# Convolution taps on the vector engine: their place in the issue order behind operations of their own step

## The chip, the cores and the metric

The kernel runs on one core of a Trainium2 chip. Its time is the device time of one execution in microseconds (us). Three runs of the kernel before gave 1438.69, 1437.74 and 1432.52 us; the median is 1437.74 us. TensorE (PE in the profile) multiplies matrices into PSUM, VectorE (DVE) and ScalarE (ACT) empty PSUM and do elementwise work, GpSimd (POOL) does elementwise work in SBUF, SyncE (SP) issues most DMAs. Each engine runs its own instructions in the order in which they were put into its program.

## The reference, cut to what matters

The kernel computes a two-layer block on 512 tokens (and 256 context tokens in its first layer), followed by a second block with two attentions and a mixture of 32 experts. Only the two layers of the first block are touched. In each of them a wide input projection of the normalised tokens feeds an attention branch and two convolution branches, which an output projection joins again:

```python
parts = split_in(h @ w_in[l])
q = mla_q(parts[0], ...)
k, v = mla_kv(parts[1], parts[2], ...)
attn = attend(q, concat([kc, k]), concat([vc, v]))          # 8 heads
y_a = attn * silu(g_a)
y_b = sc_b * dwconv(sc_c * sc_in, sc_conv_w) * silu(g_b)    # 3 taps
z = dwconv(a * sigmoid(g), cf_conv_w) + cf_conv_b           # 31 taps, 256 channels
z = silu(layer_norm(z, cf_ln_w, cf_ln_b))
y_c = (z @ cf_pw_w + cf_pw_b) * silu(g_c)
x_new = x + gate * (concat([y_a, y_b, y_c]) @ w_out[l])
```

Layer 0 does this for 768 rows (512 tokens and 256 context rows), layer 1 for 512 rows and uses the context for keys and values only. All of it is float32; a large product is three matmuls of a high and a low part of each factor (`mm3`, lines 219 to 221), so most operands are split first: ACT makes the high part, DVE the low one (`split`, lines 182 and 183).

## The kernel before, in words

The 256 channels of the 31-tap convolution are two tiles `zp` of 128 channels each. A tap is one DVE instruction over a whole row (783 columns in layer 0, 512 in layer 1): line 566 for the first tap, line 569 for the other thirty, which multiply a shifted row by a weight column and add the sum so far, `za`. So a layer has 62 taps, and the taps of one tile form a chain. They go into a list `taps` when the projection `cf_g` of their tile is done, and `tick(n)` takes n of them from the list and writes them into the program.

A layer has two loops around them. The **token loop** runs over six tiles of 128 rows. For each it projects keys, values and queries, takes their norms (`rsq`, ten small DVE operations in a chain, lines 231 to 240), scales the keys `kt` (line 850) and the queries `qt` (line 855) and stores both to DRAM. In between, `early.run` hands out matmuls of eight projections: `cf_a` and `cf_g` of both tiles and the four attention gates `g_a`. A gate's PSUM bank is emptied by a tanh on ACT (line 528) and a multiply on DVE (line 529). These projections use two PSUM banks in turn. After each tile stands `tick(TA)`, and one more after the loop. The list is empty in the first tile; it gets its first taps in the second.

The **attention loop** runs over (head, group of 256 queries): 24 steps in layer 0, 16 in layer 1. A step takes scores (`pS`), their maximum on DVE (line 917), the exponential on ACT, the reciprocal on DVE, a multiply on POOL (line 921), transposes on TensorE and a split of each into two parts (lines 182 and 183), and the product with the values in `pO`. It ends with the DVE operation `ot` (line 965), which adds the two halves of `pO`, and with a POOL multiply into `oa` (line 966). `late.run` hands out matmuls of ten further projections (the 3-tap branch, the gates `g_b` and `g_c`, one PSUM bank) and of the modulation weights. Then stands `tick(TB)`. From three quarters of the steps on (step 18 and step 12, counted from 0) `tick(99)` writes all taps that are left, and the layer norm of the convolution begins (`norm_conv`, its first matmul `pmean` on line 637).

In this part of the kernel the order on each engine isn't the order of the text. A scheduler goes through the whole block with modelled durations and gives each engine, when it is free, the earliest instruction of the text that is ready by its model. So a tap that is ready can be put ahead of much that stands before it in the text, whenever DVE would have to wait for that. The order is fixed at build time; on the chip each engine just follows it. In the second block PE's order is written by hand (`manual_schedule`), in places ACT's and DVE's too.

Of the kernel before, what the change touches and what calls it, by code (L numbers as in the profile page):

```python
# [15 lines left out]
OP = mybir.AluOpType  # L16
# [64 lines left out]
        self.debt = min(self.debt, 2.0)  # L81


TA, TB, PB, LNS = 3, 2, 4, 0.75
FP = (0.9, 0.9)
FF = (0.3, 0.2, 0.3)
PTB = 3
# [23 lines left out]
class K:  # L111
# [356 lines left out]
    def layer(self, l, hT, wl):  # L468

        nc, I, sp, tc = self.nc, self.I, self.sp, self.tc  # L470
# [24 lines left out]
        for nm in ("q_head_norm_w", "k_head_norm_w"):  # L495
            w = self.brow(tr, I[nm][l][64:96], 32, "w32" + nm[0])
            t = tr.tile([128, 4, 2, 32], F32, name="tab" + nm[0])
# [40 lines left out]
        za, zs, taps = [None] * 2, [None] * 2, []  # L538
# [32 lines left out]
            taps.extend((tap, k) for k in range(31))  # L571

        def tick(n):
            for _ in range(min(n, len(taps))):
                f, k = taps.pop(0)
                f(k)

        def g_a(i):
            yield from cm(416 + i * 128, gate2(oa[:, i, :NTOK]), self.p1)
# [104 lines left out]
        for t in range(6):  # L684
            if t < 5:
                parts[t + 1] = self.qkv_cT(t + 1, *lat[t + 1][:2], tr, qnw, kvnw, last)
            self.qkv_tile(l, t, lat[t][0], lat[t][2], parts[t], tr, qtm, ktm, vtm, tabs, last)
            early.run(8 * sum(n for _, n in segs) / 800 * 4 / 3)
            tick(TA)
        early.run(1e9)  # L690
        tick(TA)
        tr.release()

# [9 lines left out]
        n = len(mods) // 4  # L703
# [29 lines left out]
        for s, (h, g) in enumerate(steps):  # L733
            if g == 0 and h + 1 < H:
                prep[h + 1] = self.mla_prep(h + 1, ap, qtm, ktm, vtm, qk, last)
            out = self.mla_out(h, g, prep[h][0], Ps, ap, oa)
            if s + 1 < len(steps):
                h1, g1 = steps[s + 1]
                if g1 == 0:
                    for _ in prep[h1][1]:  # L740
                        pass
                Ps = self.mla_scores(prep[h1][0], g1, ap)
            next(out)
            sh = each * (0.5 if g == 2 else 1.0)
            late.run(sh * FF[0])
            for _ in out:
                late.run(sh * FF[1])
            if h + 1 < H:
                for _ in range(2):
                    next(prep[h + 1][1], None)  # L750
            late.run(sh * FF[2])
            if last and s % 2:
                self.table_rows(s // 2)
            tick(TB)
            late.level()
            if g == ngr - 1 and h % 2:
                halves.append(h // 2)
            over = not (late.gens or late.ready)
            if s >= len(steps) * LNS and (over or stage < 4):
                tick(99)  # L760
                next(ln, None)
                stage += 1
            if over:
                next(tail, None)
                for i in halves:
                    self.split(hT[0][:, i, :NTOK], hT[1][:, i, :NTOK], oa[:, i, :NTOK])
                halves = []
# [42 lines left out]
    def qkv_tile(self, l, t, L, kss, cT, tr, qtm, ktm, vtm, tabs, last):  # L810
        nc, sp = self.nc, self.sp
        isx = t < 4
        doq = isx or not last
        ch, cl = cT
        st = sp.tile([128, 16], F32, name="hst", bufs=2)
        kt = tr.tile([128, 8, 96], F32, name="kt", tag="kt", bufs=2)
        vs = tr.tile([128, 8, 64], F32, name="vs", tag="vs", bufs=1)
        pk = self.pa("pkv")
        for s in range(2):
            self.mm3(pk[:, s * 512:(s + 1) * 512], (ch[:, 2], cl[:, 2]),  # L820
                     [w[:, s * 512:(s + 1) * 512] for w in self.wukv], True, True)
        pkv = pk.rearrange("p (h n) -> p h n", h=8)
        nc.scalar.activation(kt[:, :, 0:64], pkv[:, :, 0:64], AF.Copy)
        nc.scalar.activation(vs, pkv[:, :, 64:128], AF.Copy)
        nc.sync.dma_start(vtm[t].rearrange("p (h n) -> p h n", h=8), vs)
        if doq:
            qt = tr.tile([128, 8, 96], F32, name="qt", tag="qt", bufs=2)
            pq = self.pa("pq")
            for c0, c1 in ((0, 512), (512, 768)):
                for k in range(2):  # L830
                    self.mm3(pq[:, c0:c1], (ch[:, k], cl[:, k]), [w[:, c0:c1] for w in self.wuq[k]], k == 0, k == 1)
            nc.scalar.activation(qt, pq[:, :768].rearrange("p (h n) -> p h n", h=8), AF.Copy)
        sk = tr.tile([128, 768], F32, name="sq", tag="sq", bufs=2)[:, :512].rearrange("p (h n) -> p h n", h=8)
        nc.scalar.activation(sk, kt[:, :, 0:64], AF.Square)
        nc.vector.tensor_reduce(st[:, 8:16], sk, axis=AX.X, op=OP.add)
        nc.vector.tensor_scalar(st[:, 8:16], st[:, 8:16], kss, None, op0=OP.add)
        r = sp.tile([128, 16], F32, name="hr", bufs=2)
        if doq:
            sqq = tr.tile([128, 768], F32, name="sq", tag="sq", bufs=2).rearrange("p (h n) -> p h n", h=8)
            nc.scalar.activation(sqq, qt, AF.Square)  # L840
            nc.vector.tensor_reduce(st[:, 0:8], sqq, axis=AX.X, op=OP.add)
            self.rsq(r, st, 1.0 / 96, EPS)
        else:
            self.rsq(r[:, 8:16], st[:, 8:16], 1.0 / 96, EPS)
        kr = L[:, 384:416]
        if isx:
            kk = sp.tile([128, 2, 32], F32, name="krot", bufs=2)
            self.rope_op(kk, kr[:, None, :], tabs[1][:, t], 1, tr)
            kr = kk[:, 0, :]
        nc.vector.tensor_tensor(kt[:, :, 0:64], kt[:, :, 0:64], r[:, 8:16, None].to_broadcast([128, 8, 64]), op=OP.mult)  # L850
        nc.gpsimd.tensor_tensor(kt[:, :, 64:96], kr[:, None, :].to_broadcast([128, 8, 32]),
                                r[:, 8:16, None].to_broadcast([128, 8, 32]), op=OP.mult)
        nc.sync.dma_start(ktm[t].rearrange("p (h n) -> p h n", h=8), kt)
        if doq:
            nc.vector.tensor_tensor(qt, qt, r[:, 0:8, None].to_broadcast([128, 8, 96]), op=OP.mult)
            if isx:
                self.rope_op(None, qt[:, :, 64:96], tabs[0][:, t], 8, tr)
            nc.sync.dma_start(qtm[t].rearrange("p (h n) -> p h n", h=8), qt)
# [66 lines left out]
    def mla_out(self, h, g, qkv, Ps, ap, oa):  # L925

        nc = self.nc
        v = qkv["v"]
        nj = 2 if g == 2 else 6
        def tr(j):  # L930
            p = self.pt("pPT").rearrange("p (j n) -> p j n", j=2)
            for jj in range(2):
                for i in range(2):
                    nc.tensor.transpose(p[:, jj, i * 128:(i + 1) * 128], Ps[i][:, (j + jj) * 128:(j + jj + 1) * 128],  # L934
                                        self.ident)
            x = [ap.tile([128, 2, 256], F32R, name="PT" + k, tag="PT" + k, bufs=PTB) for k in "hl"]
            self.split(*x, p)
            return x

        def pv(j, x):  # L940

            for k in range(2):
                for jj in range(2):
                    nc.tensor.matmul(pO, v[:, (4 if g == 2 else 0) + j + jj, :], x[k][:, jj, :],
                                     start=(j + k + jj == 0), stop=(j + 2 == nj and k + jj == 2))

        pO = self.po("pO")[:, :256]
        t0 = tr(0)
        if g == 2:
            yield  # L950
            pv(0, t0)
        else:
            t1 = tr(2)
            yield
            pv(0, t0)
            t2 = tr(4)
            yield
            pv(2, t1)
            yield
            pv(4, t2)  # L960
        b = (h % 2) * 64
        o = oa[b:b + 64, h // 2, g * 256:(g + 1) * 256]
        t = ap.tile([128, 256], F32, name="ot", tag="ot", bufs=2)[b:b + 64]
        nc.scalar.activation(t, pO[64:128], AF.Copy)
        nc.vector.tensor_tensor(t, pO[0:64], t, op=OP.add)  # L965
        nc.gpsimd.tensor_tensor(o, o, t, op=OP.mult)  # L966


# [1197 lines left out]
```

## Time and profile before

| | |
|---|---|
| median of three runs | 1437.74 us |
| the profiled execution's own time | 1439.8 us |
| its span, first to last instruction | 1437.7 us |
| TensorE busy | 1315.5 us, 92% of the span |
| VectorE busy | 951.7 us, 66% |
| ScalarE busy | 610.1 us, 42% |
| GpSimd busy | 313.4 us, 22% |
| mean granted TensorE clock | 0.968 of full speed |

The span is that of one execution taken by the profiler, with 2.1 us of its time outside the span. Busy shares are means over very different stretches: the token loops of the two layers lie at about 75 to 165 us and 530 to 593 us, the attention loops at about 180 to 415 us and 605 to 765 us, the second block from about 800 us on. The rows named below are read stretch by stretch for that reason.

### The profile page before, as it was taken

What the parts mean: (1) busy time and instruction counts of PE and PEld (TensorE: products, weight loads), DVE (VectorE), ACT (ScalarE), POOL (GpSimd) and SP (SyncE); (2) the same over time, 40 slices, a digit from 0 to 9 for tenths busy, and PEclk for the clock granted to TensorE, in tenths of its full rate; (3) what the DMA queues carried; (4) which work ended last, traced back from release to release, by engine and by line L of the source; (5) the groups of instructions that cost most, each with busy time, mean ns of one, the idle gap of its engine ahead of it and who ended that gap; (6) DMA issues with size and microseconds to landing.
All of it is one profiled execution on the core that took longest, in us unless ns stands there. A gap on an engine that the chain in (4) does not pass through costs nothing. (4 is left out here: it accounts for less than half of the span.)

```text
span 1437.7 us, 22499 instructions
## 1 busy us (share of the span) xinstructions
PE 1315.5 (92%) x8030; PEld 1044.9 (73%) x8030; DVE 951.7 (66%) x2123; ACT 610.1 (42%) x1195; POOL 313.4 (22%) x414
## 2 busy tenths in 40 slices
PE   4999999989989999799999999999997999999873
PEld 3888788877868788678877787887776877675441
DVE  5789997666633789997683646666667443444555
ACT  4543264545531564266573336767553111112111
POOL 5332033322220333143231201111111121111100
PEclk9999999999999999999999999999997999999987
DMA  9643364444132435434233455224545699999971
GB/s 346 150 137 103 100 169 124 129 137 144 63 123 73 116 108 156 125 87 116 69 120 131 151 177 132 77 72 138 171 174 190 222 303 359 378 369 386 389 286 59
DMA packets 167317, 246.45 MB, mean 171 GB/s; under 512 B 47267, under 2 KB 103289, under 8 KB 167205
## 3 DMA queue, kind: packets, MB, share of 16 engines
q1 hardware_dynamic: 161116, 234.95, 49.7%
q0 software_dynamic: 5408, 7.93, 2.1%
q10 hardware_dynamic: 680, 2.13, 0.4%
q8 instruction: 64, 1.05, 0.3%
q14 instruction: 49, 0.39, 0.1%
HBM read 221.74 MB, written 33.33 MB: 177 GB/s over the span
## 5 line engine op out<-in xcount | busy, mean ns | idle before, releaser
L183 DVE TENSOR_TENSOR wlo<-wraw,whi 128x1024 fp32r<-128x1024 f32 (+3 forms) x98 | 118.2, 1212 | 59.3 <-ACT whi L182 58.7
L182 ACT ACTIVATE whi<-wraw 128x1024 fp32r<-128x1024 f32 (+3 forms) x98 | 100.6, 1036 | 102.0 <-PE pout L221 42.7
L219 PE MATMUL pcm<-hTh,whi 128*128 128x256 f32 (+1 forms) x288 | 102.9, 357 | 9.3 <-DVE oa L529 4.3
L569 DVE SCALAR_TENSOR_TENSOR za<-zp,vec,za 128x783 f32<-128x783 f32 (+1 forms) x120 | 108.8, 914 | 0.5
L921 POOL TENSOR_SCALAR P<-P,ll 128x768 f32<-128x768 f32 (+1 forms) x80 | 73.4, 922 | 159.8 <-DVE ll L920 144.9
L221 PE MATMUL pcm<-hTh,wlo 128*128 128x256 f32 (+1 forms) x288 | 99.1, 344 | 0.1
L220 PE MATMUL pcm<-hTl,whi 128*128 128x256 f32 (+1 forms) x288 | 98.6, 342 | 0.0
L183 DVE TENSOR_TENSOR PTl<-pPT,PTh 128x512 fp32r<-128x512 f32 x104 | 70.3, 684 | 28.2 <-ACT PTh L182 27.8
L182 ACT ACTIVATE PTh<-pPT 128x512 fp32r<-128x512 f32 x104 | 60.6, 595 | 47.6 <-PE pPT L934 43.4
L919 ACT ACTIVATE P<-pS,nm 128x768 f32<-128x768 f32 (+1 forms) x80 | 64.9, 814 | 37.4 <-DVE nm L917 31.1
L1810 POOL DMA_INDIRECT xg<-h2d,tok x32 | 31.5, 984 | 209.2 <-PE pturn L1794 131.2
L1416 POOL TENSOR_SCALAR P<-P,l 128x384 f32<-128x384 f32 (+1 forms) x64 | 33.2, 532 | 184.7 <-DVE l L1415 167.6
L917 DVE TENSOR_REDUCE nm<-pS 128x1 f32<-128x768 f32 (+1 forms) x80 | 66.0, 843 | 10.9 <-PE pS L221 10.2
L219 PEld LDWEIGHTS pcm<-hTh,whi 128*128 128x128 f32 x288 | 55.2, 192 | 17.5 <-DVE oa L529 4.9
L219 PE MATMUL pcm<-hT0h,whi 128*128 128x512 f32 x144 | 59.3, 412 | 7.7 <-DVE oa L529 5.8
L934 PE MATMUL pPT<-ident,P 128*128 128x128 f32 x416 | 63.3, 281 | 0.9 <-DVE PTl L183 0.4
L1827 PE MATMUL pgu<-exT,eraw 128*128 128x128 f32 x512 | 61.8, 281 | 0.0
L1827 PEld LDWEIGHTS pgu<-exT,eraw 128*128 128x128 f32 x512 | 60.3, 197 | 1.1 <-DVE exT L1805 0.6
L221 PEld LDWEIGHTS pcm<-hTh,wlo 128*128 128x128 f32 x288 | 55.1, 191 | 6.8 <-DVE wlo L183 0.8
L966 POOL TENSOR_TENSOR oa<-oa,ot 64x256 f32<-64x256 f32 x40 | 37.4, 936 | 102.6 <-DVE ot L965 99.3
L220 PEld LDWEIGHTS pcm<-hTl,whi 128*128 128x128 f32 x288 | 55.3, 192 | 5.1 <-issue 0.5
L220 PE MATMUL pcm<-hT0l,whi 128*128 128x512 f32 x144 | 58.4, 406 | 0.0
(552 smaller groups left out, 3681.6 us busy)
## 6 DMA issues: line engine op xcount, KB each, us to landing
wraw<-in_w_in_dram SPq DMA_DIRECT2D x56, 512.0 KB
eraw<-in_w_expert_gate_dram SPq DMA_DIRECT2D x52, 512.0 KB
eraw<-in_w_expert_up_dram SPq DMA_DIRECT2D x52, 512.0 KB
wraw<-in_w_mod_dram SPq DMA_DIRECT2D x48, 512.0 KB
wl<-in_w_expert_down_dram SPq DMA_DIRECT2D x32, 512.0 KB
wh<-in_w_expert_down_dram SPq DMA_DIRECT2D x32, 512.0 KB
wraw<-in_w_out_dram SPq DMA_DIRECT2D x24, 512.0 KB
wraw<-in_w_expert_gate_dram SPq DMA_DIRECT2D x12, 512.0 KB
```

What stands on the lines that cost most here:

```text
L182: nc.scalar.activation(hi, src, AF.Copy)
L183: return (eng or nc.vector).tensor_tensor(lo, src, hi.bitcast(F32), op=OP.subtract)
L219: mm(out, lhs[0], rhs[0], start=start, stop=False)
L220: mm(out, lhs[0], rhs[1], start=False, stop=False)
L221: mm(out, lhs[1], rhs[0], start=False, stop=stop)
L569: nc.vector.scalar_tensor_tensor(a[:, :nz], z[:, k:k + nz], cfw[:, i, k:k + 1], a[:, :nz], op0=OP.mult, op1=OP.add)
L917: nc.vector.tensor_reduce(nm, S, axis=AX.X, op=OP.max, negate=True)
L919: nc.scalar.activation(P, S, AF.Exp, bias=nm, accum_out=l)
L921: nc.gpsimd.tensor_scalar(P, P, l, 0.5, op0=OP.mult, op1=OP.mult)
L934: nc.tensor.transpose(p[:, jj, i * 128:(i + 1) * 128], Ps[i][:, (j + jj) * 128:(j + jj + 1) * 128], self.ident)
L966: nc.gpsimd.tensor_tensor(o, o, t, op=OP.mult)
L1827: self.last = self.nc.tensor.matmul(p[:, s, c, :], gu[2 * s + k // 4][:, k % 4, c * 128:(c + 1) * 128], x[:, k, :], start=(k == 0), stop=( ...
```

## The change: what it does

Three edits go together. The DVE operations on lines 850 (`kt`) and 965 (`ot`) are kept as `self.mark`. `tick` writes its taps in a block `tc.issue_after(self.mark.ins)`: each DVE instruction written there gets an edge to the mark that holds in the issue order alone, with no semaphore and no wait for the mark's end. So the taps of a tick can stand on DVE only behind the last `kt` or `ot` written so far. And the counts change: four taps a token tile instead of three, two an attention step in layer 0 as before, and three instead of two in layer 1.

```diff
-TA, TB, PB, LNS = 3, 2, 4, 0.75
+TA, TB, PB, LNS = 4, (2, 3), 4, 0.75
...
         def tick(n):
-            for _ in range(min(n, len(taps))):
-                f, k = taps.pop(0)
-                f(k)
+            with tc.issue_after(self.mark.ins):
+                for _ in range(min(n, len(taps))):
+                    f, k = taps.pop(0)
+                    f(k)
...
-            tick(TB)
+            tick(TB[l])
...
-        nc.vector.tensor_tensor(kt[:, :, 0:64], kt[:, :, 0:64], r[:, 8:16, None].to_broadcast([128, 8, 64]), op=OP.mult)
+        self.mark = nc.vector.tensor_tensor(kt[:, :, 0:64], kt[:, :, 0:64], r[:, 8:16, None].to_broadcast([128, 8, 64]), op=OP.mult)
...
-        nc.vector.tensor_tensor(t, pO[0:64], t, op=OP.add)
+        self.mark = nc.vector.tensor_tensor(t, pO[0:64], t, op=OP.add)
```

No instruction is added or taken away, and no shape, buffer or DMA is changed.

## Rows read from the trace of the kernel before

**Rows 1.** The page's first part: busy us (share of the span) and instructions.
```profile
PE 1315.5 (92%) x8030; PEld 1044.9 (73%) x8030; DVE 951.7 (66%) x2123; ACT 610.1 (42%) x1195; POOL 313.4 (22%) x414
```

**Rows 2.** Busy us by stretch: length, PE, PEld, DVE, ACT, POOL, granted clock, DMA.
```profile
95.00:182.00 87.00, 81.16 (x447) 68.91 (x446) 84.84 (x143) 27.73 (x48) 20.23 (x19) 0.98 0.34 106
187.00:226.00 39.00, 38.13 (x273) 31.79 (x272) 36.81 (x68) 22.58 (x49) 15.11 (x19) 1.00 0.53 147
226.00:359.00 133.00, 126.41 (x894) 104.80 (x894) 83.91 (x159) 69.29 (x144) 37.88 (x43) 0.99 0.46 134
545.00:605.00 60.00, 52.66 (x227) 41.97 (x225) 57.62 (x120) 21.08 (x34) 13.88 (x16) 0.94 0.45 138
602.00:645.00 43.00, 41.76 (x265) 33.04 (x263) 39.56 (x65) 22.89 (x45) 14.02 (x14) 1.00 0.32 76
645.00:736.00 91.00, 89.42 (x551) 72.82 (x550) 67.85 (x115) 57.06 (x110) 28.86 (x30) 1.00 0.38 102
```

**Rows 3.** One line's instructions: taps up to 163.6, 194.7, 592.9, 621; `ot` by layer.
```profile
L569 DVE SCALAR_TENSOR_TENSOR za<-zp,vec,za x38: 1014/1022/1396, 98.5 to 162.2; 128x783 f32<-128x783 f32 x38
L569 DVE SCALAR_TENSOR_TENSOR za<-zp,vec,za x52: 1012/1023/1396, 98.5 to 188.6; 128x783 f32<-128x783 f32 x52
L569 DVE SCALAR_TENSOR_TENSOR za<-zp,vec,za x32: 735/742/1018, 546.0 to 592.2; 128x512 f32<-128x512 f32 x32
L569 DVE SCALAR_TENSOR_TENSOR za<-zp,vec,za x50: 731/741/1100, 546.0 to 619.6; 128x512 f32<-128x512 f32 x50
L965 DVE TENSOR_TENSOR ot<-pO,ot x24: 405/417/419, 194.7 to 413.0; 64x256 f32<-64x256 f32 x24
L965 DVE TENSOR_TENSOR ot<-pO,ot x16: 403/417/419, 621.0 to 764.3; 64x256 f32<-64x256 f32 x16
```

**Rows 4.** PE's timeline: start us, duration, what ran, in brackets the idle time before it.
```profile
127.78 0.50 PE L219 MATMUL pcm<-hTh,whi 128*128 128x512 f32 x1 [1.07 <-DVE oa L529]
...
141.49 0.50 PE L219 MATMUL pcm<-hTh,whi 128*128 128x512 f32 x1 [1.32 <-DVE oa L529]
...
163.70 0.73 PE L219 MATMUL pcm<-hTh,whi 128*128 128x512 f32 x1 [1.93 <-DVE oa L529]
...
167.21 0.41 PE L221 MATMUL pcm<-hTh,wlo 128*128 128x512 f32 x1
...
588.82 0.80 PE L219 MATMUL pcm<-hT0h,whi 128*128 128x512 f32 x1 [5.79 <-DVE oa L529]
...
594.01 0.39 PE L219 MATMUL pcm<-hT0h,whi 128*128 128x512 f32 x1
594.25 0.40 PE L220 MATMUL pcm<-hT0l,whi 128*128 128x512 f32 x1
```

**Rows 5.** ACT's and DVE's timelines: the tanh and the multiply ahead of two waits.
```profile
161.81 0.38 ACT L528 ACTIVATE oa<-pcm 128x256 f32<-128x256 f32 x1 [2.12 <-PE pcm L221]
...
163.23 0.42 DVE L529 SCALAR_TENSOR_TENSOR oa<-oa,pcm 128x256 f32<-128x256 f32 x1
...
583.79 0.58 ACT L528 ACTIVATE oa<-pcm 128x512 f32<-128x512 f32 x1
...
588.09 0.68 DVE L529 SCALAR_TENSOR_TENSOR oa<-oa,pcm 128x512 f32<-128x512 f32 x1
```

**Rows 6.** Busy us by stretch, as in rows 2, behind the two longest waits.
```profile
163.00:168.00 5.00, 4.30 (x12) 3.43 (x13) 4.93 (x8) 0.00 (x0) 0.61 (x1) 0.66 0.44 158
586.50:594.00 7.50, 5.18 (x12) 4.10 (x13) 7.50 (x19) 0.00 (x0) 1.59 (x1) 0.54 0.43 136
```

**Rows 7.** DVE's timeline: taps in a row, one group in each layer.
```profile
165.41 4.23 DVE L569 SCALAR_TENSOR_TENSOR za<-zp,vec,za 128x783 f32<-128x783 f32 x4
...
593.46 8.39 DVE L569 SCALAR_TENSOR_TENSOR za<-zp,vec,za 128x512 f32<-128x512 f32 x12
```

**Rows 8.** Groups by line on POOL, 187 to 226 us, then 226 to 359 us.
```profile
L921 POOL TENSOR_SCALAR P<-P,ll 128x768 f32<-128x768 f32 x7 | 7.3, 1047 | 5.6 <-DVE ll L920 5.5
...
L921 POOL TENSOR_SCALAR P<-P,ll 128x768 f32<-128x768 f32 x20 | 18.3, 916 | 35.7 <-DVE ll L920 28.0 <-PE pcm L221 4.1 <-DVE mod L337 3.0
```

**Rows 9.** One line's instructions: the first matmuls of the layer norm in layer 1.
```profile
L637 PE MATMUL pmean<-za,ones x4: 591/592/592, 729.7 to 736.9; 128*128 128x512 f32 x4
```

## The prediction

> **What bounds the kernel now.** I read the page's busy shares first. TensorE is busy for 92% of the span and DVE for 66% [rows 1], so TensorE's order of work sets the end and DVE counts only where TensorE waits for it. Then the busy times by stretch, because the mean hides two kinds of stretches. In the token loops and just behind them DVE is busy for 84.84 of 87 us in layer 0 and 57.62 of 60 in layer 1, and TensorE has its holes there: 5.84 and 7.34 us without a matmul [rows 2]. In the attention loops DVE has room (83.91 of 133 us, 67.85 of 91) and TensorE is busy for 95% and 98%. Third, the taps by line: 52 of layer 0's 60 on line 569 and 50 of layer 1's have begun before the first `ot`, at 194.7 and 621.0 us [rows 3]; with the two first taps of a layer that makes 54 and 52 of 62. By the text only 18 of a layer (six ticks of three) belong to the token loop. So DVE is full there because the scheduler pulled the taps forward into each small gap of the norm's chain. Fourth, TensorE's timeline: its four longest waits for DVE there, 1.07, 1.32, 1.93 and 5.79 us, are all for the multiply `oa` of line 529, which empties a projection's PSUM bank [rows 4]. That multiply stood behind taps.
>
> **The change part by part.** It removes no work. It moves taps: with six ticks of four, 24 of a layer stay with the token loop (the last four behind the last `kt`) and 38 go behind an `ot`. Against the counts of rows 3, 54 - 24 = 30 taps of layer 0 and 52 - 24 = 28 of layer 1 move behind the first `ot`. A tap in a row of taps costs 4.23 / 4 = 1.06 us in layer 0 and 8.39 / 12 = 0.70 in layer 1 [rows 7]. So 31.8 + 19.6 = 51 us of DVE work move out of the full stretches into the attention loops. A tap issues no DMA, so nothing of it stands in SP's or POOL's queue; only the stores of `kt` and `qt`, on SP, can come earlier.
>
> What goes, layer 0. Before the wait of 1.93 us the tanh of that bank ended at 161.81 + 0.38 = 162.19, and the multiply started at 163.23 [rows 5]: 1.0 us of it was DVE's queue, the rest is the hand-over from engine to engine, which stays. The waits of 1.07 and 1.32 I take whole (between nothing, if a tap of the tile's own tick still stands there, and the whole). Sum 3.4. The matmuls behind the third wait ran at a granted clock of 0.66 on average [rows 6], that is partly at 1.2 and not 2.4 GHz: eight matmuls from 163.70 to 167.21, 0.44 us each, where at full clock one takes 594.25 - 594.01 = 0.24 [rows 4]. That is 3.51 - 1.92 = 1.6 us. The clock of the whole stretch is 0.98 [rows 2], 2% of 87 us, about 3.5 us at half clock: this one drop and none behind the waits of 1.07 and 1.32. So I take the 1.6 as saved when 0.9 is left of the third.
>
> What goes, layer 1. The tanh ended at 583.79 + 0.58 = 584.37, the multiply could have started then and started at 588.09 [rows 5]: I take 3.5 of the 5.79 us. Twelve matmuls from 588.82 to 594.01 took 5.19 us where 12 x 0.24 = 2.9 would have done: 2.3 us of slow clock, which I leave in the sum because 2.3 us of waiting remain and the wait of 1.93 was already followed by a slow stretch. Its bounds are 0 and 2.3.
>
> So the token loops give 3.4 + 1.6 + 3.5 = 8.5 us, 10.8 with the last clock term, and nothing if the taps of a tick (four in a row, 4.23 us) stand before these multiplies again. I take 8.5: up to the last `kt` the two loops held 38 + 2 = 40 and 32 + 2 = 34 taps [rows 3], and now 20 each.
>
> What comes, attention loops. The taps of a step stand earlier in the text than the next step's DVE work, so they run right behind `ot`: 2 x 1.06 = 2.1 us in layer 0, 3 x 0.70 = 2.1 us in layer 1, over 19 and 13 steps. Behind them in DVE's queue wait the next splits of transposes, the score maxima and the splits of weights; TensorE waits for those unless projections fill the time. In layer 0, 38 x 1.06 = 40.3 us are spread over about 164 us (194.7 to 359), so the 133 us from 226 on, which held no tap but the last two, get some 32.7 us: 83.91 + 32.7 = 116.6, 88% of DVE. In layer 1, 38 x 0.70 = 26.6 us over about 115 us (621 to 736) give the 91 us from 645 on 21.0 us: 67.85 + 21.0 = 88.9, 98%. The nearest rows are the two stretches in which taps already ran beside attention: DVE at 36.81 / 39 = 94% with TensorE at 98%, and 39.56 / 43 = 92% with TensorE at 97% [rows 2]. So layer 0 costs nothing as long as projections cover it, and layer 1 asks for more than any row shows beside a full TensorE: if DVE gets to 92% as there, the 88.9 us take 96.6 instead of 91, 5.6 us more; if it can be filled, nothing. I take 3.
>
> The POOL multiply on line 921 is the one step of the softmax chain that taps could slow without standing before it in a queue. It took 1.047 us on average where taps ran beside it and 0.916 where nearly none did [rows 8]: 0.13 us, twice a step, over 32 steps 8.4 us of POOL time, on an engine busy for 38 of 133 us. I price it at nothing and leave those 8.4 us to the slower rival.
>
> The Trainium skill (SBUF — State Buffer, section Who interferes with whom) speaks against the change here: it says that a DVE instruction with two SBUF inputs, as a tap is, contends with a GpSimd instruction that reads SBUF, and that the later of the two is held back until the first is done. By that rule alone each of 64 multiplies could wait for a whole tap, an estimate of 38 x 1.06 + 26 x 0.70 = 58 us on the softmax chain; the trace shows the effect with 0.13 us, and the measurement decides.
>
> The ends of the chains. Layer 1's last two taps stand behind the `ot` of step 12 (735.8 us before), so `za` is whole at about 738, where its last `pmean` matmul ran at 736.9 [rows 9]: about 1 us later, in a chain that goes on only with the next steps. Nothing. The second tile's `zp` buffer is taken over by the second gate `g_c`, whose projection comes after that step in the text as well: nothing, unless the scheduler had wanted it earlier.
>
> One gain is not a wait of today: with `rsq` no longer interleaved with taps, the last `kt` and `qt` come earlier and attention starts with less of its projections used up, so more of them are left for its end. Between 0 and the 133 - 126.41 = 6.6 us in which TensorE runs nothing from 226 to 359 [rows 2]; I take 2, as most of that is other engines' latency.
>
> Sum: 8.5 - 3 + 2 = 7.5 us less. From the profiled execution, 1439.8 - 7.5 = 1432.3; that execution lies 2.1 us above the median of 1437.74, so against the median the forecast is **1430**.
>
> **The rivals.** *The gain is given back.* The multiplies of line 529 wait anyway, now for the block of four, or layer 1's full DVE returns what its token loop gave: 8.5 - 5.6 - 2 leaves 1, **1436**. For it: 98% of DVE in layer 1's steps. Against it: layer 1's block of four takes only 2.8 us, and 14 taps fewer stand in its token loop.
>
> *Slower: DVE's blocks sit in the softmax chain.* In 32 steps the chain from scores to `pO` gets 2.1 us longer, 67 us together. TensorE covers that with projections; where 30% of it is not covered, 20 us come, and 1437.7 - 8.5 + 20 = **1449**. It decides from (8.5 + 7.2) / 67 = 23% on. For it: layer 1's 98%, and the 0.13 us of line 921. Against it: TensorE at 97% and 98% in the stretches where taps ran beside attention.
>
> *It does not do what it says.* The order is only held from below: if four taps a tile are again spread between the ten `rsq` operations, the token loop keeps its holes, and only the counts change: **1438**.
>
> **How the numbers follow.** The measurement can tell about 0.5% from no change, 7.2 us: faster is below 1430.5, slower above 1444.9. My forecast lies at the edge of that. Forecast and better: 0.46. Given back: 0.27, and no effect 0.10, both within the bound. Slower: 0.17. The forecast's own range is 1420 (a gain of 10.8 + 6.6) to 1435; the range that leaves out 2 in 10 goes up to 1442, towards the slower case and short of it.
>
> **What would show it.** In the changed profile: at most four taps between two `kt`, none before the first `ot` beyond 24; the waits for line 529 under 1 us each and the granted clock at 1.00 in 163 to 168; DVE under 85% in both token loops. In attention: DVE near 88% and 98% in the stretches from 226 and 645 us, TensorE still at 95% or more. I am wrong if TensorE's waits for line 183 or 917 in the attention loops grow by more than 8 us together, or if the waits for line 529 stay.

## The result: 1.2% slower, and the profile after

The changed kernel took 1453.95 us (median of four runs, 1452.93 to 1454.95), the kernel before 1436.2 beside it (four runs, 1432.52 to 1438.69): a ratio of 1.0123, with an interval of 1.0102 to 1.0143. The forecast was 1430 us. The profiled execution took 1453.46 us. Its page against [rows 1]: the same instructions, and 13 us more of DVE and 17 of POOL.

```profile
PE 1315.0 (91%) x8030; PEld 1038.5 (72%) x8030; DVE 964.7 (66%) x2123; ACT 613.2 (42%) x1195; POOL 330.3 (23%) x414
```

To see where the time went I cut each layer at instructions that both kernels have: from the first `kt` to the first `ot` (token loop) and from the first `ot` to the last (attention loop). Both traces read so, columns as in [rows 2]; first the kernel before, layer 0's two stretches and then layer 1's:

```profile
79.65:194.68 115.03, 108.85 (x617) 93.01 (x616) 106.91 (x185) 42.15 (x77) 33.17 (x34) 0.99 0.40 120
194.68:413.00 218.32, 206.04 (x1379) 169.59 (x1378) 146.97 (x279) 113.91 (x232) 60.27 (x71) 0.96 0.43 129
531.00:620.96 89.96, 82.50 (x382) 66.79 (x381) 85.07 (x170) 35.26 (x60) 28.06 (x34) 0.96 0.41 123
620.96:764.29 143.33, 139.31 (x853) 113.34 (x853) 113.59 (x196) 86.83 (x166) 46.02 (x45) 0.96 0.37 100
```

The changed kernel, the same four stretches:

```profile
81.23:184.50 103.27, 100.04 (x569) 85.51 (x568) 84.05 (x153) 42.02 (x76) 32.37 (x34) 0.98 0.42 130
184.50:420.19 235.69, 214.59 (x1427) 175.94 (x1426) 177.70 (x312) 115.16 (x233) 73.81 (x71) 0.97 0.40 120
538.22:622.87 84.65, 75.94 (x351) 60.93 (x349) 70.48 (x137) 35.15 (x60) 28.43 (x32) 0.94 0.44 131
622.87:778.70 155.83, 144.93 (x884) 114.80 (x885) 133.85 (x228) 88.67 (x166) 50.79 (x47) 1.00 0.33 92
```

By their lengths the token loops won 11.8 and 5.3 us and the attention loops lost 17.4 and 12.5. Most of this is TensorE work that changed places: the token loops have 8.8 and 6.6 us less of it, the attention loops 8.6 and 5.6 more. Length less PE busy separates that from idle time. TensorE's idle time went from 6.2 to 3.2 and from 7.5 to 8.7 us in the token loops, and from 12.3 to 21.1 and from 4.0 to 10.9 us in the attention loops. The four together are 12.8 us longer: idle 29.9 to 43.9, so 14.0 more, and 1.2 less of matmuls. The span is 13.8 us longer, so nearly all of the loss is here.

The taps stand where the change puts them. These are the groups of line 569 in the changed kernel, up to the first `ot` and from there on, in layer 0 and then in layer 1, to be read against [rows 3]:

```profile
L569 DVE SCALAR_TENSOR_TENSOR za<-zp,vec,za x23: 1017/1034/1399, 100.0 to 165.3; 128x783 f32<-128x783 f32 x23
L569 DVE SCALAR_TENSOR_TENSOR za<-zp,vec,za x37: 1015/1020/2295, 185.4 to 370.7; 128x783 f32<-128x783 f32 x37
L569 DVE SCALAR_TENSOR_TENSOR za<-zp,vec,za x23: 734/752/1228, 553.2 to 602.0; 128x512 f32<-128x512 f32 x23
L569 DVE SCALAR_TENSOR_TENSOR za<-zp,vec,za x37: 730/737/1176, 624.3 to 755.9; 128x512 f32<-128x512 f32 x37
```

With the two first taps of a layer that is 24 and 38, as worked out. In layer 0's token loop DVE has room now (74.00 of 87 us from 95 to 182 us). What did not come is room in layer 1's token loop and a DVE as full in attention as forecast. The changed kernel in three of the stretches of [rows 2]:

```profile
226.00:359.00 133.00, 120.38 (x853) 98.55 (x851) 100.81 (x174) 63.67 (x133) 46.28 (x41) 0.99 0.44 128
545.00:605.00 60.00, 52.21 (x223) 41.94 (x222) 54.89 (x111) 21.28 (x33) 18.81 (x19) 0.91 0.54 163
...
645.00:736.00 91.00, 86.91 (x544) 68.59 (x543) 76.84 (x125) 49.96 (x94) 30.97 (x27) 1.00 0.40 106
```

DVE is at 54.89 / 60 = 91% in layer 1's token loop. In attention it is at 100.81 / 133 = 76% from 226 us on and at 84% from 645, where the prediction had 88% and 98%. So TensorE lost time beside a DVE that had 24% and 16% of its time free.

### The profile page after: what moved, and what is told of

Its sections match the earlier page's. It is cut to its first block, busy times and chain, and to the rows that moved or that the text cites. A ratio compares the mean times of both kernels' runs of the same rounds, so it can differ in the third digit from the quotient of the medians.

```text
span 1451.5 us, 22479 instructions
## 1 busy us (share of the span) xinstructions
PE 1315.0 (91%) x8030; PEld 1038.5 (72%) x8030; DVE 964.7 (66%) x2123; ACT 613.2 (42%) x1195; POOL 330.3 (23%) x414
## 5 line engine op out<-in xcount | busy, mean ns | idle before, releaser
L569 DVE SCALAR_TENSOR_TENSOR za<-zp,vec,za 128x783 f32<-128x783 f32 (+1 forms) x120 | 114.9, 957 | 1.3
L920 ACT ACTIVATE P<-pS,nm 128x768 f32<-128x768 f32 (+1 forms) x80 | 64.9, 814 | 42.5 <-DVE nm L918 31.2
L967 POOL TENSOR_TENSOR oa<-oa,ot 64x256 f32<-64x256 f32 x40 | 56.8, 1420 | 103.1 <-DVE ot L966 101.3
L219 PEld LDWEIGHTS pcm<-hTh,whi 128*128 128x128 f32 x288 | 55.0, 191 | 12.3 <-DVE oa L529 3.1
L219 PE MATMUL pS<-khi,qhi 96*128 96x256 f32 (+1 forms) x144 | 51.7, 359 | 8.3 <-ACT P L920 6.1
## 6 DMA issues: line engine op xcount, KB each, us to landing
eraw<-in_w_expert_up_dram SPq DMA_DIRECT2D x52, 512.0 KB, 10.9
wh<-in_w_expert_down_dram SPq DMA_DIRECT2D x32, 512.0 KB, 10.9
```

What stands on the lines that cost most here:

```text
L219: mm(out, lhs[0], rhs[0], start=start, stop=False)
L569: nc.vector.scalar_tensor_tensor(a[:, :nz], z[:, k:k + nz], cfw[:, i, k:k + 1], a[:, :nz], op0=OP.mult, op1=OP.add)
L920: nc.scalar.activation(P, S, AF.Exp, bias=nm, accum_out=l)
```

## Where the waits went

**Token loops.** Two of the four waits of [rows 4] are still there. The changed kernel's PE timeline at the two places:

```profile
163.35 0.63 PE L219 MATMUL pcm<-hTh,whi 128*128 128x512 f32 x1 [2.14 <-DVE oa L529]
...
598.23 0.80 PE L219 MATMUL pcm<-hT0h,whi 128*128 128x512 f32 x1 [7.24 <-DVE oa L529]
```

They were 1.93 and 5.79 us. The first two, 1.07 and 1.32, left one of 0.57. ACT's timeline of the changed kernel has the tanh ahead of the later multiply:

```profile
591.77 0.58 ACT L528 ACTIVATE oa<-pcm 128x512 f32<-128x512 f32 x1
```

DVE's timeline of the changed kernel shows what stood in front of both:

```profile
161.93 1.03 DVE L569 SCALAR_TENSOR_TENSOR za<-zp,vec,za 128x783 f32<-128x783 f32 x1
162.88 0.41 DVE L529 SCALAR_TENSOR_TENSOR oa<-oa,pcm 128x256 f32<-128x256 f32 x1
...
593.95 0.69 DVE L851 TENSOR_TENSOR kt<-kt,hr 128x512 f32<-128x512 f32 x1
594.56 1.89 DVE L569 SCALAR_TENSOR_TENSOR za<-zp,vec,za 128x512 f32<-128x512 f32 x2
596.36 1.22 DVE L183 TENSOR_TENSOR wlo<-wraw,whi 128x1024 fp32r<-128x1024 f32 x1
597.50 0.68 DVE L529 SCALAR_TENSOR_TENSOR oa<-oa,pcm 128x512 f32<-128x512 f32 x1
```

In layer 1 the tanh ended at 592.35 and the multiply began 5.15 us later, behind the rest of the norm's chain, `kt`, two taps of its tile's tick (1.89 us) and a split of weights (1.22 us). Before, it began 588.09 - 584.37 = 3.7 us late [rows 5].

**Attention loops.** TensorE's waits in layer 0's steps, summed by what it waited for (total us, times, longest). The kernel before, 207 to 360 us, most of its loop:

```profile
PE pS L219 <- ACT P L919: 2.3, 4, 0.9
PE pO L944 <- DVE PTl L183: 0.7, 2, 0.4
PE pO L944 <- ACT PTh L182: 0.4, 2, 0.2
```

The changed kernel, 195 to 372 us:

```profile
PE pS L219 <- ACT P L920: 4.9, 6, 1.9
...
PE pO L945 <- ACT PTh L182: 2.1, 3, 1.4
...
PE pO L945 <- DVE PTl L183: 1.4, 2, 1.1
```

These are the links of the softmax chain, and each is longer. The waits that name line 183 are the smaller part: over both attention loops they grew from 3.0 to 7.5 us, those of `pS` and `pO` for ACT's exponential `P` and high part `PTh` from 4.0 to 10.0. One step shows how. DVE's timeline in the changed kernel, from one `ot` on:

```profile
231.19 0.42 DVE L966 TENSOR_TENSOR ot<-pO,ot 64x256 f32<-64x256 f32 x1 [0.29 <-ACT ot L965]
231.64 1.19 DVE L569 SCALAR_TENSOR_TENSOR za<-zp,vec,za 128x783 f32<-128x783 f32 x1
232.75 1.08 DVE L183 TENSOR_TENSOR vhl<-vraw,vhl 128x384 fp32r<-128x384 f32 x1
233.76 1.02 DVE L569 SCALAR_TENSOR_TENSOR za<-zp,vec,za 128x783 f32<-128x783 f32 x1
234.70 1.80 DVE L918 TENSOR_REDUCE nm<-pS 128x1 f32<-128x768 f32 x2
236.43 1.27 DVE L183 TENSOR_TENSOR PTl<-pPT,PTh 128x512 fp32r<-128x512 f32 x2
```

PE's timeline of the changed kernel has the wait that ends it:

```profile
237.16 0.50 PE L945 MATMUL pO<-PTl,vhl 128*128 128x256 f32 x2 [1.09 <-DVE PTl L183]
```

Both taps stand ahead of the score maxima `nm` and of the split `PTl`, on which the next product waits. DVE has idle time in this loop, 24% from 226 to 359 us, but a tap that must stand behind this `ot` can use none of what lies ahead of it, and is itself ahead of what comes next.

## The experiments

The edits are against the changed kernel unless the text says otherwise. The table has the ratio to the kernel before, with its interval, and from each profile TensorE's idle time (length less PE busy) in the four stretches, and the time from the first `kt` of layer 0 to the last `ot` of layer 1.

| kernel | ratio | token 0 | attention 0 | token 1 | attention 1 | first `kt` to last `ot` |
|---|---|---|---|---|---|---|
| before | | 6.2 | 12.3 | 7.5 | 4.0 | 684.6 |
| changed | 1.0123 (1.0102 to 1.0143) | 3.2 | 21.1 | 8.7 | 10.9 | 697.5 |
| counts only | 1.0015 (0.9991 to 1.0039) | 6.2 | 12.5 | 8.5 | 5.4 | 685.6 |
| attention taps held | 1.0106 (1.0069 to 1.0144) | 3.4 | 19.8 | 7.3 | 10.6 | 691.0 |
| token taps held | 1.0095 (1.0058 to 1.0132) | 8.7 | 13.6 | 9.2 | 5.4 | 694.3 |
| held by the last `kt` | 1.0097 (1.0063 to 1.0131) | 4.6 | 17.2 | 7.6 | 6.2 | 689.3 |
| one step later | 1.0040 (1.0020 to 1.0059) | 3.9 | 16.7 | 8.4 | 6.1 | 684.0 |
| no attention taps | not comparable | 3.3 | 12.4 | 8.4 | 4.9 | 679.4 |
| before, banks exchanged | 1.0014 (0.9998 to 1.0030) | 4.5 | 13.9 | 5.3 | 5.7 | 680.2 |
| changed, banks exchanged | 1.0080 (1.0055 to 1.0104) | 1.2 | 19.0 | 5.2 | 10.8 | 689.9 |
| one step later, banks exchanged | 1.0014 (0.9995 to 1.0032) | 1.5 | 17.8 | 5.2 | 7.6 | 680.8 |

The last column is one execution, and it holds chance: the kernel before with its banks exchanged is 4.4 us shorter there than the kernel before, and no faster by its runs. Idle time and the ratios are read first for that reason.

**Counts, and each hold alone.** `tick` gets a switch, one for the token loop and one for the attention loop:

```diff
+HT, HA = False, False
...
-        def tick(n):
-            with tc.issue_after(self.mark.ins):
+        def tick(n, held=True):
+            with tc.issue_after(self.mark.ins) if held else ExitStack():
...
-            tick(TA)
+            tick(TA, HT)
...
-            tick(TB[l])
+            tick(TB[l], HA)
...
-                tick(99)
+                tick(99, HA)
...
-        tick(99)
+        tick(99, HA)
```

Counts only, both switches off:

> The counts of the change (4 a tile; 2 and 3 a step) with no taps queued behind a mark at all. If the holding costs the time (theory), this is the kernel before again: ratio to before 0.996 to 1.004, taps run early, waits for line 529 of about 10 us in the token loops. If the counts themselves cost it (rival: more taps a step), it is 1.006 or more.

Measured: 1440.32 us (ten runs) beside 1435.49, 1.0015. The counts cost nothing that can be told from the noise, so the loss belongs to the holds.

Attention taps held alone (`HA = True`):

> Only the taps of attention steps are queued behind their step's ot; those of the token loop are free. Theory (each step's taps stand in the softmax chain of the next steps): the attention loops lose some 17 and 12 us against before as in the changed kernel, the token loops gain part of what they gained there; ratio to before 1.008 to 1.016. Rival (the loss is a new order that the scheduler happened on, not the taps' place): the loss is gone or halved, ratio under 1.005.

Measured: 1452.07, 1.0106. That is as much as the whole change within the intervals, and the same shape: layer 0's token loop is as short (103.3 us) and the attention loops are nearly as long (230.1 and 155.4 us). So the first `ot` comes early because the attention steps' taps may no longer be pulled ahead of it. The hold on `kt` has no part in that.

Token taps held alone (`HT = True`):

> Taps of the token loop queued as in the changed kernel, those of attention steps not queued at all, so the second tile's 31 taps can still run in the token loop as soon as their input is there. Theory: a smaller gain in the token loops than with all held behind the last kt, no loss in attention; ratio to before 0.992 to 1.000. Rival (any DVE work more in attention costs): between 1.000 and 1.008.

Measured: 1449.96, 1.0095, outside both expected ranges. Here the attention steps' taps are free, and the scheduler pulls them forward: 54 of line 569's taps have begun by 197.7 us, ahead of the first `ot` at 201.1. The taps of the token tiles may not fill the gaps ahead of their `kt`, and DVE stays full. The stretch of this kernel:

```profile
79.70:201.11 121.41, 112.67 (x628) 96.02 (x627) 110.24 (x185) 41.95 (x75) 34.71 (x33) 0.96 0.36 114
```

That is its layer 0 token loop, columns as in [rows 2]. Against the first of the four stretches of the kernel before it is 6.4 us longer, with 2.6 us more idle. Attention stays near the kernel before (13.6 and 5.4 us of idle). The idle time of the four stretches is 7.1 us more than before, spread over all of them; why held token taps beside free attention taps cost that much is not shown. The two holds do not add up to the change: each alone costs most of it, at other places.

**Held by the last `kt` alone.** The mark is no longer set at `ot`, so the attention steps' taps stand behind the last `kt` and may use any gap from there on:

```diff
-        self.mark = nc.vector.tensor_tensor(t, pO[0:64], t, op=OP.add)
+        nc.vector.tensor_tensor(t, pO[0:64], t, op=OP.add)
```

> Taps of the token loop queued as in the changed kernel; those of attention steps only behind the last kt of the token loop, so from there on they run wherever the scheduler finds a gap. Theory (place within the step): the token loops keep their gain of about 10 and 5 us, the attention loops lose little; ratio to before 0.988 to 0.997. Rival (any 51 us of DVE work more in the attention loops costs that time): ratio 1.006 to 1.015, as in the changed kernel.

Measured: 1449.53 (1446.36 to 1453.65), 1.0097. I had expected it to be faster than the kernel before, and that is refuted; the ratio lies where the rival had it, by which any added DVE work in attention costs time. Two thirds of the added idle time of layer 1's attention is gone (6.2 instead of 10.9), but layer 0's attention is idle for 17.2 us against 12.3. At its start 15 taps of line 569 stand between 162 us and the first `ot` at 193.1 us. TensorE is idle there for 3.5 of 31.2 us, which is no more than before (29.12 of 32.68 us busy up to its first `ot`), but its granted clock is 0.84, a mix of its two levels of 1.2 and 2.4 GHz, where it was 0.95. That stretch of this kernel:

```profile
162.00:193.15 31.15, 27.69 (x137) 21.00 (x138) 25.37 (x41) 11.72 (x27) 6.17 (x6) 0.84 0.46 133
```

All four stretches together have 5.7 us more idle than before, in a profile of 1446.44 us, one of the shortest of this kernel's five runs. Its median is 14 us above the kernel before, so the larger part of this loss has no place in the trace that I can name.

**One step later.** The taps of a step stand behind the `ot` of the step before. The number of taps of each tick is that of the change; only the edge is looser:

```diff
-        def tick(n):
-            with tc.issue_after(self.mark.ins):
+        def tick(n, m=None):
+            with tc.issue_after((m or self.mark).ins):
...
-            tick(TB[l])
+            tick(TB[l], self.prev)
...
-                tick(99)
+                tick(99, self.prev)
...
+        self.prev = self.mark
         self.mark = nc.vector.tensor_tensor(t, pO[0:64], t, op=OP.add)
```

> The changed kernel, but the taps of a step are queued behind the ot of the step before, so they come after the step's own operations in the text and only fill gaps of DVE; their number a step is the same. Theory of the place (they cost because they run right behind ot, ahead of the softmax chain): at least half of the loss in attention is gone, ratio 1.000 to 1.006, and idle time in steps 4 to 18 of layer 0 near 8 us. Rival (what counts is how many taps run beside attention): ratio 1.008 to 1.015, idle near 13 us.

Measured: 1442.56 us (ten runs, 1439.75 to 1448.24) beside 1437.8, 1.0040. Two thirds of the loss are gone ((1.23 - 0.40) / 1.23) with the same taps in the same loop. Its attention loops, columns as in [rows 2]:

```profile
186.55:414.60 228.05, 211.36 (x1416) 173.95 (x1416) 176.49 (x310) 114.40 (x233) 72.20 (x71) 0.98 0.40 123
...
617.88:765.39 147.51, 141.44 (x875) 115.03 (x875) 130.82 (x223) 87.18 (x166) 51.69 (x47) 0.99 0.35 97
```

DVE works in attention as much as in the changed kernel (176.49 and 130.82 us there, 177.70 and 133.85 with the change), and the attention loops are 7.6 and 8.3 us shorter. So most of the cost is the place of the taps, and not their number. DVE's timeline of this kernel in the same step:

```profile
229.91 0.42 DVE L967 TENSOR_TENSOR ot<-pO,ot 64x256 f32<-64x256 f32 x1 [0.29 <-ACT ot L965]
230.36 1.33 DVE L569 SCALAR_TENSOR_TENSOR za<-zp,vec,za 128x783 f32<-128x783 f32 x1
231.62 1.08 DVE L183 TENSOR_TENSOR vhl<-vraw,vhl 128x384 fp32r<-128x384 f32 x1
232.62 1.81 DVE L918 TENSOR_REDUCE nm<-pS 128x1 f32<-128x768 f32 x2
234.35 0.68 DVE L183 TENSOR_TENSOR PTl<-pPT,PTh 128x512 fp32r<-128x512 f32 x1
...
235.17 0.69 DVE L183 TENSOR_TENSOR PTl<-pPT,PTh 128x512 fp32r<-128x512 f32 x1
235.78 1.24 DVE L569 SCALAR_TENSOR_TENSOR za<-zp,vec,za 128x783 f32<-128x783 f32 x1
```

The second tap went behind both splits `PTl`. They were done 5.95 us after the start of `ot` (235.17 + 0.69 - 229.91), in the changed kernel 6.51 us after it (236.43 + 1.27 - 231.19). That is 0.56 us in this step. The first product that needs a `PTl` starts 5.17 us after the start of `ot` (235.08 - 229.91) instead of 5.97 (237.16 - 231.19), and TensorE waits 0.30 us for it instead of 1.09:

```profile
235.08 0.51 PE L945 MATMUL pO<-PTl,vhl 128*128 128x256 f32 x2 [0.30 <-DVE PTl L183]
```

Over the 32 steps of both layers that have taps the looser edge took back 9.2 us of idle time in attention ((21.1 - 16.7) + (10.9 - 6.1)), of the 15.7 that the change added.

**No attention taps.** 37 of the 38 taps that a layer has left after its token loop are not computed (the first tap of the second tile stays). The convolution's result is another, tokens go to other experts, and the second block is some 38 us longer; only the first block is compared:

```diff
         late = Fill(late)
+        taps[:] = [x for x in taps if x[1] == 0]
```

> The changed kernel with 37 of the 38 taps of the attention steps of each layer left out (the convolution's sum is incomplete). Theory (taps behind ot cost TensorE some 13 us of waiting): TensorE's idle time falls to about 6.6 us in steps 4 to 18 of layer 0 and 1.5 us in steps 4 to 12 of layer 1, where the changed kernel has 13.1 and 5.0; 12 to 20 us less than the changed kernel, ratio to before 0.990 to 1.003. Rival (the new order costs it, whether the taps run or not): ratio 1.006 or more.

Measured: 1475.31 us in all; from the first `kt` to the last `ot` 679.4 us, 18.1 less than the changed kernel and 5.2 less than the one before. The attention loops of this kernel:

```profile
185.31:410.11 224.80, 212.43 (x1426) 175.74 (x1426) 142.15 (x274) 114.50 (x233) 58.63 (x71) 0.97 0.41 127
611.20:761.35 150.15, 145.25 (x883) 118.71 (x884) 108.60 (x191) 87.20 (x166) 44.79 (x47) 0.97 0.34 95
```

Idle is 12.4 and 4.9 us, within 1 us of the kernel before, with the same deferred projections as in the changed kernel. So the taps behind `ot` make the added idle time, and the deferral does not. Against the kernel before, with 74 taps fewer, only 1.0 of the 5.2 us is idle time in the four stretches; most of the rest is TensorE's busy time (532.6 against 536.7 us), which one profile can't tell from chance.

**The port rival.** A DVE tap and a GpSimd operation run side by side in the changed kernel more often, since the multiply on line 966 (967 there) is released by the same `ot` as the taps. I left that multiply out, of the kernel before and of the changed one; the attention branch then stays at its gate alone and tokens go to other experts, so again the first block is compared first:

```diff
-        nc.gpsimd.tensor_tensor(o, o, t, op=OP.mult)
```

> The kernel before with the same multiply left out, to compare with. Both theories: 0.995 to 1.001 of the kernel before, since that multiply is on no chain of TensorE.

> The changed kernel without GpSimd's multiply of attention output and gate behind each ot (left out). Taps right behind ot then meet no GpSimd read. Theory of the shared port (the taps and GpSimd hold each other up): taps of layer 0 in attention fall from 1.15 to about 1.04 us, and this kernel gains 5 us or more against the same cut of the kernel before. Rival (DVE's queue alone): the taps get shorter, and the distance to the same cut of the kernel before stays at 13 to 18 us.

Measured, from the first `kt` to the last `ot`: 678.2 us without the change and 690.1 with it. The change costs 11.9 us there without the multiply and 12.8 with it. By idle time in the four stretches it costs 10.3 us (29.6 to 40.0) and 14.0 with the multiply, and by the whole kernels 14.1 us (1582.47 and 1596.59, medians of four runs) and 17.8. So the three readings leave this contention 1 to 4 us of the loss, less than the 5 that its theory asked for and too little to be told from the noise of four runs. Most of the loss stays without the multiply. The whole kernels lie far above the ratio expected without the multiply, as their second block is longer with the tokens at other experts.

**The waits for line 529.** The forecast's gain was these waits. To take them away otherwise, the two PSUM banks of the projections change places in layer 0, which carries on into layer 1. This is one line before `early = Fill(...)`, added to the kernel before, to the changed one, and to that of the later step:

```diff
+        self.np1 += l == 0
```

> The kernel before with the two PSUM banks of the early projections in the other order, so that the last gate of the token loop no longer sits in the one bank that the first projection of attention needs. Theory (the waits of 1.93 and 5.79 us and the slow clock behind them hang on that bank, whatever taps do): both are gone, ratio 0.991 to 0.997. Rival (DVE's queue full of taps is what holds TensorE there): a wait of 3 us or more moves to another matmul, ratio 0.998 to 1.002.

> Taps queued behind the ot of the step before, with the banks in the other order as well. Theory: the waits of 2.1 and 7.2 us at the end of the token loops, which the changed kernel kept, go with the bank; ratio to before 0.990 to 0.998, below the lagged taps alone (1.004). Rival: they stay, ratio 1.002 to 1.006.

> The changed kernel with the banks in the other order. Theory: 4 to 8 us less than the changed kernel, ratio to before 1.006 to 1.010, the loss in the attention loops unchanged. Rival (the wait at the end of the token loops is DVE's queue): no gain, ratio 1.011 to 1.014.

Measured, in the kernel before: 1438.84 us (twelve runs) beside 1438.1, 1.0014 (0.9998 to 1.0030). In layer 1 the wait for line 529 shrinks from 5.8 to 0.2 us, and another one comes. PE's waits in layer 1's token loop of this kernel (total us, times, longest):

```profile
PE pcm L219 <- DVE u L603: 4.3, 1, 4.3
...
PE pcm L219 <- DVE oa L529: 0.2, 1, 0.2
```

And the stretch itself, columns as in [rows 2]:

```profile
530.16:619.55 89.39, 84.13 (x389) 68.17 (x388) 84.71 (x169) 35.28 (x60) 27.96 (x34) 0.96 0.41 124
```

The stretch is 0.6 us shorter than before. DVE has the same 85 us of work in it, and the next bank that DVE empties waits for the same taps. Over both token loops idle time falls by 3.9 us, over both attention loops it rises by 3.3.

With the changed kernel the exchange gives 1449.73, 1.0080 (1.0055 to 1.0104), as the theory expected: about 0.4% less than 1.0123. Here no other wait for DVE of that size comes; layer 1 has one of 3.5 us for the load of the first keys instead (`kraw`). The two token loops of this kernel:

```profile
80.72:181.72 101.00, 99.85 (x579) 85.53 (x578) 84.48 (x154) 43.00 (x76) 32.41 (x34) 1.00 0.42 129
...
533.57:615.09 81.52, 76.31 (x364) 61.44 (x362) 72.53 (x141) 35.30 (x60) 29.21 (x34) 1.00 0.45 136
```

TensorE is idle for 1.2 and 5.2 us in them, 6.4 instead of the 13.6 before the change, at a granted clock of 1.00. So held taps and the exchange together bring 7.3 us, about the 6.9 that the forecast had booked for the waits; the attention loops stay as slow as with the change alone (19.0 and 10.8 us idle). With the later step the exchange gives 1439.48, 1.0014 (0.9995 to 1.0032), between the two expected ranges. No kernel beat the one before.

## Why the prediction was wrong

The forecast's sum was -8.5 (token loops), -2 (projections left over) and +3 (attention loops). The step that failed is the last: "layer 0 costs nothing as long as projections cover it", and 3 us for layer 1.

**The attention loops cost 15.7 us of idle TensorE, not 3.** Layer 0, priced at nothing, lost 8.8 and layer 1 lost 6.9. The price came from DVE's share of a stretch: 94% and 92% beside a full TensorE [rows 2], so there seemed to be room. The taps were no sparser there: 8.99 of 39 us and 13.80 of 43, where the sum put 32.7 into 133 and 21.0 into 91. But in those rows the taps stood wherever the scheduler's model had DVE idle, that is, behind what the chain needed. The change pins them ahead of it. Rows about a filler in gaps do not price the same filler at the head of the queue. The counts-only kernel and the one with the later edge show that difference with the taps themselves kept. The slower rival had the mechanism right: its 67 us of added chain, of which 15.7 us or 23% were not covered, about the point from which it was to decide. It ended above its 1449 because the other side of the sum was smaller too. Of the two signs of being wrong the second came true. The first did not: waits named for lines 183 and 917 grew by 4.5 us and not by 8, because more of the growth, 6.0 us, was in the waits for ACT's `P` and `PTh`.

**The token loops gave 1.7 us of idle, not 6.9 and 1.6 of clock.** The waits of 1.07 and 1.32 became one of 0.57, but the third and the fourth stayed and grew, as the first rival had it ("now for the block of four"): a tap stood ahead of the one and two taps ahead of the other. The mistake was to count fewer taps in the loop and conclude that none stands in front of this multiply. No clock came back either: the granted clock from 163 to 168 us is 0.66 in both kernels, and 0.98 and 0.94 over the two token loops where it was 0.99 and 0.96. What was missing is shown by the exchange of banks in the changed kernel: with it the waits for line 529 are 0.6 and 0.5 us, and the token loops win what the sum had for them.

**A named wait was taken for a gain.** The exchange of banks took layer 1's wait away without the change and won nothing that can be measured: beside a full DVE (84.71 of 89.39 us) a wait of 4.3 us came at the next bank. Beside the emptier DVE of the changed kernel (72.53 of 81.52) the same exchange was worth 7.7 us of idle time over the four stretches.

**Projections left over gave nothing, not 2 us.** 8.8 and 6.6 us of TensorE work did move from the token loops into the attention loops, as the step said. But with them in place and no taps in the attention loops (the kernel without attention taps), idle there is 17.3 us against 16.3 before.

**What held.** The counts of 24 and 38 taps and the hold itself were right, so the third rival is out. The multiply on line 921 was rightly priced at nothing: the changed kernel's 64 wide ones take 977 ns on average from 170 to 790 us, where they took 1010 before. The end of the convolution cost nothing that I can see: layer 1's last `pmean` matmul began at 757.3 us instead of 736.9 [rows 9], in a loop 14.4 us later by its last `ot`, and only 1.5 us of waiting is for `pmean`, put down to ACT. Two slips in the prediction change nothing: the stretch from 226 us held the end of one tap, the last, which began at 225.4, and not two; and 1 us off 1437.74 is 1437, not 1436.

**What stays open.** The kernel with the later edge is 0.4% slower than the one before. Its profile has 5.1 us more idle in the four stretches, which would be all of that, but the same profile is as short as the one before from the first `kt` to the last `ot`, with less PE busy time; it is one of the shortest of that kernel's ten runs. I did not separate the two. So the last third of the loss may be the price of any added DVE work in attention. The kernels with the token taps held and with the hold by the last `kt` point that way or to something else: each loses about 1% without a tap pinned behind an `ot`.

## What to carry to other kernels

Price a filler by where it stands in its queue, not by the share of the engine: work that ran for nothing in gaps costs its latency once it is pinned ahead of the next step's chain, here half a microsecond in each of 32 steps, at 76 and 84% DVE. If fillers must be held back, use an operation early enough that the scheduler can still put the chain first; one step of slack returned two thirds of the loss here. A wait that the trace names on a full engine can go to the next bank when it is removed, as it did in the kernel before, so test it by removing it some other way before it is booked as a gain; and test it again where the engine has room, as there the same removal paid.

## What the runs showed of the hardware

The POOL multiply that joins attention and its gate (64x256, SBUF only) got much slower beside the taps. POOL's group of it from 180 to 820 us in the kernel before, busy time and mean ns behind the bar:

```profile
L966 POOL TENSOR_TENSOR oa<-oa,ot 64x256 f32<-64x256 f32 x40 | 37.4, 936 | 102.6 <-DVE ot L965 99.3 <-DVE mod L337 2.9
```

The changed kernel, the same group:

```profile
L967 POOL TENSOR_TENSOR oa<-oa,ot 64x256 f32<-64x256 f32 x40 | 56.8, 1420 | 103.1 <-DVE ot L966 101.3 <-DVE mod L337 1.4
```

It went from 936 to 1420 ns, and to 1214 with the later edge. The mean hides two kinds. In the step shown above the multiply starts behind the first tap, which ends at 231.64 + 1.19 = 232.83 us:

```profile
232.09 1.33 POOL L967 TENSOR_TENSOR oa<-oa,ot 64x256 f32<-64x256 f32 x1
```

It ends at 233.42, 0.59 us after the tap. Those of layer 0 that start 0.08 to 0.16 us behind a lone tap take 1.46 to 1.52 us and end about 0.6 us after it; the five behind the last tap take 0.73 or 0.74. The longest, 4.01 us from 263.79, spans two taps and two splits in a row and ends 0.61 us after the last of them. The taps of layer 0's attention (170 to 440 us) went from 1036 ns on average to 1147, and to 1096 where the multiply was left out. The Trainium skill (SBUF — State Buffer, section Who interferes with whom) says that a DVE instruction with two SBUF inputs contends with a GpSimd instruction that reads SBUF, over a shared port that one of them holds alone. The trace agrees: the multiply behind a tap ends only 0.6 us after the tap does. The pair without the multiply shows that little of this reached the end, 1 to 4 of the 18 us.
